# A third group of columns in seven products for eight, with two groups' sums kept in DRAM

## The chip, the cores and the metric

The kernel runs on one core of one Trainium2 chip. The metric is the device time of one execution in microseconds. TensorE (PE) multiplies, VectorE (DVE) and ScalarE (ACT) work on elements, GpSimd (POOL) and SyncE (SP) mostly issue transfers here.

## The reference

Two layers over 256 positions of width 2048, in float32. Each layer mixes positions (attention heads and gated groups, not touched here) and then runs the MLP that the change is about:

```python
h2 = rms_norm(x, norm2_g[l])
x = x + jnp.square(jax.nn.relu(h2 @ w_up[l])) @ w_down[l]
```

`w_up` is 2048 x 8192, `w_down` 8192 x 2048. After both layers a last norm is applied.

## The kernel before

**Precision and tiles.** A float32 product is made of three products of a reduced format: the high part of the weight with the high part of the other operand, low with high, high with low. Every 512 KB of weights is a tile `raw` of 128 x 1024; ScalarE copies it to its high part `hi` (L160) and VectorE subtracts that from `raw` to get the low part `lo` (L170). `x` is kept transposed, as 128 rows of 16 chunks.

**Steps.** The program is one list `steps`, and the loop at the end of `trunk` issues it: for each step the high and low parts of later tiles (low parts up to four tiles ahead of the step's first, with six `lo` and seven `hi` buffers), then loads, then the step's matmuls, then what follows it. A plain step of `transposed` (L391, L393, L395) takes one tile in 24 matmuls of 256 columns. `later` and `soon` put a piece of work off until so many tiles are done; `hook` ties one to a step. Each engine runs its own instructions in the order in which this loop issues them.

**The MLP.** It runs in rounds e = 0 to 8, called eighths here. Up to e = 7, eighth e makes 1024 hidden columns in 16 plain steps (0 to 15); every fourth step ends two chunks, which VectorE scales and clips (L733), ScalarE squares (L734) and both split into `half` (L629, L630). From e = 1 on, it also multiplies the hidden columns of e - 1 with 1024 rows of `w_down`, and `update` (L489) adds the result to `x`. A plain column block of 256 takes two plain steps.

**Seven products for eight.** A group is 512 of the 2048 output columns. `fast` multiplies its 1024 rows as a 2 x 2 block product with seven half-size products instead of eight (a Strassen-Winograd form). It takes two fast steps in each eighth, each with four tiles: two loaded (`Top`, `Bottom`) and two that VectorE makes from them (`Sums`, L210 to L214, written over the loaded ones). The hidden side needs sums too: `sums` (L747 to L750) and their splits (L629, L630 into `shared`). A fast step issues 36 matmuls; six of its seventh product are left to the step behind it (`left_over`).

Group 0 uses `fast` in all eight eighths and keeps its products in the four `aux` banks until the end. Group 1 uses it in eighths 1 to 7: two banks (`acc2`, `acc3`) and the free half bank hold five products all the time, and the sixth and seventh share whatever accumulator is free (`spare`), which is added up in SBUF in each eighth (`kept`, L803 and L805). When a group is complete, `combine` (L762 to L769) makes four blocks of the products and `turn_back` (L778) transposes them for `update`.

**The order around the change** is a table of positions: in eighths 2 to 7 the group 1 pair stands before steps 1 and 2, the group 0 pair before 6 and 13, and eight plain steps of `w_down` end the eighth:

```python
            at = {1: (7, 10, 14, 15), 8: (0, 2)}.get(e, (6, 13, 1, 2))
            for i, one in enumerate(rest):
                if quick and i in at:
                    steps.append(quick[at.index(i)])
                steps.append(one)
            if up:
                steps.extend(down)
```

Weights are loaded by SP; each load waits until the `lo` part of an earlier tile is made. POOL has nothing to do in the MLP.

Of the kernel before, what the change touches and what calls it, by code (L numbers as in the profile page):

```python
# [35 lines left out]
P = 128  # L36
# [4 lines left out]
NH = 8  # L41
# [19 lines left out]
FAST = (512, 512)  # L61
# [24 lines left out]
def trunk(ctx: ExitStack, tc: tile.TileContext, layout, xT, consts, gains, w, b_sp, w_sp, out):  # L86
# [6 lines left out]
    tp = ctx.enter_context(tc.tile_pool(name="tp", bufs=1))  # L93
    pacc = ctx.enter_context(tc.tile_pool(name="pacc", bufs=1, space=bass.MemoryType.PSUM))
# [12 lines left out]
    inner = ar[:, 0:2048].rearrange("p (k t) -> p k t", k=NH)  # L107
    blocks = ar[:, 2048:2048 + 6 * 256].rearrange("p (n c) -> p n c", n=6)
    kept = ar[:, 3584:3584 + 512]
# [288 lines left out]
    def fast(name, l, row0, col0, tiles, slots, fresh, last, done):  # L398
# [3 lines left out]

        o = []
        for p in range(2):
# [3 lines left out]
            def mm(p=p, top=top, bottom=bottom, upper=upper, lower=lower):  # L408
# [7 lines left out]
                def product(n, a, lower_rows, tt, b, cols):  # L416
                    for k in range(2):
                        xh, xl = (a[:, 4 * lower_rows + 2 * p + k, i, tt * P:(tt + 1) * P] for i in range(2))
                        hi, lo = b.hi[:, k, cols], b.lo[:, k, cols]
                        pe.matmul(o[n], lhsT=xh, rhs=hi, start=(p == 0 and k == 0 and n in fresh), stop=False,  # L420
                                  skip_group_check=True)
                        pe.matmul(o[n], lhsT=xh, rhs=lo, start=False, stop=False, skip_group_check=True)  # L422
                        pe.matmul(o[n], lhsT=xl, rhs=hi, start=False, stop=(last and p == 1 and k == 1),  # L423
                                  skip_group_check=True)
# [72 lines left out]
    def layer(l, n1, n2, n3, last):  # L497
# [261 lines left out]
        def combine(o, c, banks, final):  # L759
            p1, p2, p3, p5, p7, p6, p4 = o  # L760
            b1, u, c11, c12, c21, c22 = (blocks[:, n, :] for n in range(6))
            act.activation(b1, p1, AF.Copy)  # L762
            vec.tensor_tensor(u, b1, p6, op=OP.add)
            vec.tensor_tensor(c11, b1, p2, op=OP.add)
            vec.tensor_tensor(c22, u, p7, op=OP.add)
            vec.tensor_tensor(u, u, p5, op=OP.add)
            vec.tensor_tensor(c12, u, p3, op=OP.add)
            vec.tensor_tensor(c21, c22, p4, op=OP.subtract)
            vec.tensor_tensor(c22, c22, p5, op=OP.add)  # L769
            later(2, 1.5, lambda: turn_back(c, c11, c21, banks[0], final))  # L770
            later(2, 1.5, lambda: turn_back(c + 2, c12, c22, banks[1], final))

        def turn_back(c, first, second, bank, final):
            ps = bank()
            for j in range(2):
                for tt, src in enumerate((first, second)):
                    o = j * S + tt * P
                    pe.transpose(ps[:, o:o + P], src[:, j * P:(j + 1) * P], ident)  # L778
            later(0, 1.5, lambda: update(n3, c, ps, final, last))
# [6 lines left out]
        def slots_all():  # L786
            if not held:
                held.extend(h for _ in range(4) for h in halves(aux_bank()))
            return held[0:7]

        most, spare = [], [None]

        def slots_most():
            if not most:
                most.extend(h for i in (2, 3) for h in halves(acc_bank(i)))
            spare[0] = acc_bank(1 - bank_at[0])
            return most + halves(spare[0]) + held[7:8]

        def keep(e):

            def add(o):
                if e == 1:
                    act.activation(kept, spare[0], AF.Copy)  # L803
                else:
                    vec.tensor_tensor(kept, kept, spare[0], op=OP.add)  # L805
                if e == 7:
                    later(10, 1.5, lambda: combine(o[0:4] + halves(kept) + o[6:7], FAST[0] // P,
                                                  [lambda i=i: acc_bank(i) for i in (2, 3)], False))

            return add if e == 1 else lambda o: soon(1, lambda: add(o))  # L810

        base = len(steps)
        for e in range(9):
            up, down, quick, more = [], [], [], []
            if e < 8:
                up = collect(transposed, "w_up", l, 0, KC, e * 1024, 1024, from_hs, after_up(e), of=2)
            if e:
                w = sum(FAST[:1 + (e < 8)])
# [4 lines left out]
                quick = collect(fast, "w_down", l, (e - 1) * 1024, 0, hidden, slots_all, (0, 2, 4, 6) if e == 1 else (),  # L823
                                e == 8, (lambda o: later(1, 1.5, lambda: combine(o, 0, [aux_bank] * 2, True)))
                                if e == 8 else None)
                if e < 8:
                    quick += collect(fast, "w_down", l, (e - 1) * 1024, FAST[0], hidden, slots_most,
                                     (0, 2, 4) if e == 1 else (4,), e == 7, keep(e))
            rest = up or down
            at = {1: (7, 10, 14, 15), 8: (0, 2)}.get(e, (6, 13, 1, 2))  # L830
            for i, one in enumerate(rest):
                if quick and i in at:
                    steps.append(quick[at.index(i)])
                steps.append(one)
            if up:
                steps.extend(down)
# [137 lines left out]
```

## Time and profile before

| | |
|---|---|
| median of 3 runs | 2035.96 us (2035.77 to 2036.2) |
| the profiled execution | 2035.78 us, span 2034.0 us |
| granted TensorE clock | 0.997 |
| busy: PE, DVE, ACT, POOL | 2022.0, 1539.7, 1092.9, 68.5 us |
| MLP, layer 0 | from about 333 us to 1012 us of the span |
| one steady eighth | 84.5 to 84.6 us |
| read from HBM | 390.65 MB |

Busy time of PE is a poor measure of waits, because a matmul's record (277 ns) overlaps the next; the distance from one matmul to the next tells more. The bracket at a row of a timeline gives the idle time of that engine ahead of it and what ended it. Line numbers in the profile are those of the kernel before; in the order of the changed kernel the same lines stand four or five further down (L170 is L174 there, L489 is L494).

### The profile page before, as it was taken

Reading aid. Unit: us, or ns where it says so; the run is one execution under the profiler, and the core shown is the slowest. Engines: PE = TensorE matmul, PEld = TensorE weight load, DVE = VectorE, ACT = ScalarE, POOL = GpSimd, SP = SyncE. Lnnn points to the kernel's source line nnn. Section 1 sums busy time; section 2 is a strip of 40 time slices with the busy share of each in tenths; the row PEclk is TensorE's granted clock in tenths of the full one; section 3 lists DMA queues with packets and bytes.
Section 4 is the critical chain, followed back from the end, with each engine's and each line's share of the span. In section 5 each row is a group of like instructions: output and inputs, shape, how many; then the busy total and the mean of one; then the engine's idle time right before and its main releaser. Section 6 shows DMA issues by size and latency. Waiting matters only on the chain.

```text
span 2034.0 us, 40556 instructions
## 1 busy us (share of the span) xinstructions
PE 2022.0 (99%) x16914; PEld 1985.9 (98%) x16914; DVE 1539.7 (76%) x1906; ACT 1092.9 (54%) x1389; POOL 68.5 (3%) x90
## 2 busy tenths in 40 slices
PE   9999999999999999999999999999999999999997
PEld 8998999999999999999989989999999999999997
DVE  7666766788878787788866667658887788877886
ACT  7565444555555555555645554545554655546554
POOL 0002300000000000000000032000000000000000
PEclk9999999999999999999999999999999999999998
DMA  8545556465564655646564555555565555655653
GB/s 318 190 166 167 186 189 202 170 208 197 193 231 160 225 190 193 230 162 213 187 238 157 170 183 186 187 198 169 204 203 202 208 207 184 201 196 208 207 184 107
DMA packets 112136, 395.39 MB, mean 194 GB/s; under 512 B 12368, under 2 KB 16464, under 8 KB 111952
## 3 DMA queue, kind: packets, MB, share of 16 engines
q1 hardware_dynamic: 110800, 389.86, 56.2%
q8 instruction: 132, 2.16, 0.4%
q10 hardware_dynamic: 1152, 2.94, 0.4%
q14 instruction: 52, 0.43, 0.1%
HBM read 390.65 MB, written 2.10 MB: 193 GB/s over the span
## 4 chain that ended last, share of the span: by engine, by line
PE 99%; DVE 0%; ACT 0%; issue 0%; DVEq 0%
PE acc L391 25%; PE acc L395 25%; PE acc L393 25%; PE acc L451 3%; PE acc L449 3%; PE acc L450 3%; PE aux L420 3%; PE aux L423 3%; PE aux L422 3%; PE acc L423 2%; PE acc L422 2%; PE acc L420 2%; PE aux L675 0%; PE aux L577 0%; PE aux L619 0%; PE aux L606 0%
## 5 line engine op out<-in xcount | busy, mean ns | idle before, releaser
L160 ACT ACTIVATE hi<-raw 128x1024 fp32r<-128x1024 f32 (+1 forms) x801 | 807.8, 1048 | 463.5 <-DVE raw L214 210.9
L170 DVE TENSOR_TENSOR lo<-raw,hi 128x1024 fp32r<-128x1024 f32 (+1 forms) x801 | 944.9, 1216 | 46.8 <-ACT hi L160 31.3
L391 PE MATMUL acc<-hs,hi 128*128 128x256 f32 x2816 | 780.9, 277 | 0.0
L395 PE MATMUL acc<-hs,hi 128*128 128x256 f32 x2816 | 778.0, 276 | 0.0
L393 PE MATMUL acc<-hs,lo 128*128 128x256 f32 x2816 | 778.0, 276 | 0.0
L393 PEld LDWEIGHTS acc<-hs,lo 128*128 128x128 f32 x2816 | 528.8, 188 | 0.4 <-issue 0.2
L391 PEld LDWEIGHTS acc<-hs,hi 128*128 128x128 f32 x2816 | 528.7, 188 | 0.4 <-issue 0.2
L395 PEld LDWEIGHTS acc<-hs,hi 128*128 128x128 f32 x2816 | 528.6, 188 | 0.0
L391 PE MATMUL acc<-half,hi 128*128 128x256 f32 x1600 | 442.2, 276 | 0.0
L395 PE MATMUL acc<-half,hi 128*128 128x256 f32 x1600 | 441.7, 276 | 0.0
L393 PE MATMUL acc<-half,lo 128*128 128x256 f32 x1600 | 441.7, 276 | 0.0
L393 PEld LDWEIGHTS acc<-half,lo 128*128 128x128 f32 x1600 | 300.4, 188 | 0.0
L395 PEld LDWEIGHTS acc<-half,hi 128*128 128x128 f32 x1600 | 300.4, 188 | 0.0
L391 PEld LDWEIGHTS acc<-half,hi 128*128 128x128 f32 x1600 | 300.4, 188 | 0.0
L630 DVE TENSOR_TENSOR half<-ar,half 128x512 fp32r<-128x512 f32 x72 | 49.9, 693 | 92.8 <-ACT half L629 92.8
L733 DVE SCALAR_TENSOR_TENSOR ar<-acc,nR 128x512 f32<-128x512 f32 x64 | 44.1, 689 | 91.1 <-PE acc L395 91.1
L734 ACT ACTIVATE ar<-ar 128x512 f32<-128x512 f32 x64 | 40.5, 632 | 134.2 <-DVE ar L733 134.2
L489 DVE TENSOR_TENSOR x<-x,acc 128x512 f32<-128x512 f32 (+1 forms) x89 | 60.3, 678 | 66.7 <-PE acc L395 66.7
L449 PE MATMUL acc<-hi,hs 128*128 128x512 f32 x256 | 101.5, 397 | 0.0
L451 PE MATMUL acc<-hi,hs 128*128 128x512 f32 x256 | 100.6, 393 | 0.0
L450 PE MATMUL acc<-lo,hs 128*128 128x512 f32 x256 | 99.9, 390 | 0.0
L277 ACT ACTIVATE hs<-x,cols 128x256 fp32r<-128x256 f32 x64 | 29.2, 502 | 90.8 <-DVE x L489 90.0
(150 smaller groups left out, 2253.4 us busy)
## 6 DMA issues: line engine op xcount, KB each, us to landing
raw<-in_w SPq DMA_DIRECT2D x731, 512.0 KB, 4.5
raw<-in_w SPq DMA_DIRECT2D x10, 256.0 KB, 4.7
x<-in_xT SPq DMA_DIRECT2D x7, 256.0 KB, 5.4
out<-x SPq DMA_DIRECT2D x7, 256.0 KB, 3.1
shared<-in_b_sp ACTq DMA_DIRECT2D x2, 512.0 KB, 8.2
shared<-in_w_sp ACTq DMA_DIRECT2D x2, 512.0 KB, 9.8
con<-in_consts ACTq DMA_DIRECT2D x1, 512.0 KB, 7.6
x<-in_xT ACTq DMA_DIRECT2D x2, 128.0 KB, 3.9
```

Of the source, the lines that this page charges most:

```text
L160: act.activation(self.h[:, j * m:(j + 1) * m], self.raw[:, j * m:(j + 1) * m], AF.Copy)
L170: vec.tensor_tensor(lo[:, r], self.raw[:, r], self.h[:, r].bitcast(F32), op=OP.subtract)
L391: pe.matmul(o, lhsT=hi, rhs=xs[:, 0, :], start=(k0 + k == 0 and (two or cb == 0)), stop=False, skip_group_check=True)
L393: pe.matmul(o, lhsT=wt.lo[:, k, cb * P:(cb + 1) * P], rhs=xs[:, 0, :], start=False, stop=False, skip_group_check=True)
L395: pe.matmul(o, lhsT=hi, rhs=xs[:, 1, :], start=False, stop=last, skip_group_check=True)
L420: pe.matmul(o[n], lhsT=xh, rhs=hi, start=(p == 0 and k == 0 and n in fresh), stop=False, skip_group_check=True)
L422: pe.matmul(o[n], lhsT=xh, rhs=lo, start=False, stop=False, skip_group_check=True)
L423: pe.matmul(o[n], lhsT=xl, rhs=hi, start=False, stop=(last and p == 1 and k == 1), skip_group_check=True)
L449: pe.matmul(ps, lhsT=xh, rhs=hi, start=(k0 + k == 0), stop=False)
L450: pe.matmul(ps, lhsT=xh, rhs=lo, start=False, stop=False)
L451: pe.matmul(ps, lhsT=xl, rhs=hi, start=False, stop=(k0 + k == KC - 1))
L489: vec.tensor_tensor(xj, xj, ps[j][:, 0:S] if alone else pair(ps)[:, j, :], op=OP.add)
```

## The change

Group 2 (columns 1024 to 1535) now uses `fast` too, in eighths 2 to 7. The second projection's plain steps in these eighths are four in place of eight. Group 1 no longer stays in PSUM: both groups 1 and 2 start afresh in each eighth in `acc2`, `acc3` and the accumulator that is free; when a pair is done, ScalarE copies the three banks and the half bank of the seventh product to the SBUF buffer `stage` (L845, L836), and POOL issues a DMA of 128 x 1792 numbers that adds `stage` to the group's sums in DRAM (`far`, L813). Both groups share `stage`. Group 0's seventh product goes the same way (128 x 256), since its half bank is lent to group 2. In eighth 7, group 2's sums are added from DRAM into `stage` (L840), combined and turned back; then group 1's are read (L832) and combined. Combines and turns are put off with `soon` instead of `later`.

```diff
-FAST = (512, 512)
+ORDER = {1: ((7, 10), (13, 14)), 8: ((0, 2),)}
+USUAL = ((11, 14), (1, 2), (6, 7))
...
+    dp = ctx.enter_context(tc.tile_pool(name="dp", bufs=1, space=bass.MemoryType.DRAM))
...
-    inner = ar[:, 0:2048].rearrange("p (k t) -> p k t", k=NH)
-    blocks = ar[:, 2048:2048 + 6 * 256].rearrange("p (n c) -> p n c", n=6)
-    kept = ar[:, 3584:3584 + 512]
+    inner_flat = ar[:, 0:2048]
+    inner = inner_flat.rearrange("p (k t) -> p k t", k=NH)
+    stage, stage_one = ar[:, 2048:3840], ar[:, 3840:4096]
...
+        def combine(place, c, banks, o=None, then=None):
+            d1, d2, d3, d5, d7, d6, d4 = (place[:, 256 * n:256 * (n + 1)] for n in range(7))
+            p1, p2, p3, p5, p7, p6, p4 = o or (d1, d2, d3, d5, d7, d6, d4)
+            if o:
+                act.activation(d1, p1, AF.Copy)
+            vec.tensor_tensor(d2, d1, p2, op=OP.add)
...
+            soon(2, lambda: turn_back(c, d2, d4, banks[0], o is not None))
+            soon(3, lambda: (turn_back(c + 2, d3, d7, banks[1], o is not None), then and soon(1, then)))
...
+        def slots_other(g, banks):
+            seventh = sevenths()[g - 1]
+            banks[:] = [acc_bank(2), acc_bank(3), acc_bank(1 - bank_at[0])]
+            return [h for b in banks for h in halves(b)] + [seventh]
+
+        far = [dp.tile([P, 256 if g == 0 else 7 * 256], F32, name=f"far{l}{g}") for g in range(3)]
+
+        def put(e, g, src):
+            nc.gpsimd.dma_start(far[g], src, **({} if e == max(g, 1) else {"accum_op": OP.add}))
...
+        def other_done(e, g, banks):
+            here = [lambda i=i: acc_bank(i) for i in (2, 3)]
+
+            def back():
+                nc.gpsimd.dma_start(stage, far[1])
+                soon(3, lambda: combine(stage, 4, here))
+
+            def rest(o):
+                act.activation(stage[:, 1536:1792], o[6], AF.Copy)
+                if e < 7 or g == 1:
+                    put(e, g, stage)
+                else:
+                    nc.gpsimd.dma_start(stage, far[g], accum_op=OP.add)
+                    soon(4, lambda: combine(stage, 4 * g, here, then=back if g == 2 else None))
+
+            def f(o):
+                for i in (2, 0, 1):
+                    act.activation(stage[:, 512 * i:512 * (i + 1)], banks[i], AF.Copy)
+                soon(5, lambda: rest(o))
+            return f
...
+            quick = dict(quick)
+            for i, one in enumerate(up + down):
+                if i in quick:
+                    steps.append(quick[i])
                 steps.append(one)
```

**VectorE's order from one steady eighth into the next.** Before, from the four sums on; `raw` rows are the sums of weights, `shared` the splits of the hidden sums:

```order
L747 TENSOR_TENSOR ar<-ar 128x4x128
L748 TENSOR_TENSOR ar<-ar 128x4x128
L749 TENSOR_TENSOR ar<-ar 128x4x128
L750 TENSOR_TENSOR ar<-ar 128x4x128
L170 TENSOR_TENSOR lo<-raw,hi 128x1024
L489 TENSOR_TENSOR x<-x,acc_9123 128x512
L630 TENSOR_TENSOR shared<-ar,shared 128x2x256 x2
L170 TENSOR_TENSOR lo<-raw,hi 128x1024
L630 TENSOR_TENSOR shared<-ar,shared 128x2x256 x2
L170 TENSOR_TENSOR lo<-raw,hi 128x1024
L489 TENSOR_TENSOR x<-x,acc_9193 128x512
L170 TENSOR_TENSOR lo<-raw,hi 128x1024
```

The same place now:

```order
L752 TENSOR_TENSOR ar<-ar 128x4x128
L753 TENSOR_TENSOR ar<-ar 128x4x128
L754 TENSOR_TENSOR ar<-ar 128x4x128
L755 TENSOR_TENSOR ar<-ar 128x4x128
L187 TENSOR_TENSOR lo<-raw,hi 128x512
L494 TENSOR_TENSOR x<-x,acc_9357 128x512
L635 TENSOR_TENSOR shared<-ar,shared 128x2x256 x2
L217 TENSOR_TENSOR raw<-raw 128x2x256
L218 TENSOR_TENSOR raw<-raw 128x2x256
L174 TENSOR_TENSOR lo<-raw,hi 128x1024
L635 TENSOR_TENSOR shared<-ar,shared 128x2x256 x2
L214 TENSOR_TENSOR raw<-raw 128x2x256
```

The first fast step's tiles (L187, L217, L218, L214), which came behind four more low parts and two updates, now stand among the sums and their splits.

**VectorE's order from eighth 7 into eighth 8** (layer 0). Before, this place reads as the first list above; the combine of group 1 stood earlier, behind the square that follows step 7 of eighth 7. Now, from the last of the four sums on:

```order
L755 TENSOR_TENSOR ar<-ar 128x4x128
L217 TENSOR_TENSOR raw<-raw 128x2x256
L218 TENSOR_TENSOR raw<-raw 128x2x256
L770 TENSOR_TENSOR ar<-ar 128x256
L771 TENSOR_TENSOR ar<-ar 128x256
L772 TENSOR_TENSOR ar<-ar 128x256
L773 TENSOR_TENSOR ar<-ar 128x256
L774 TENSOR_TENSOR ar<-ar 128x256
L775 TENSOR_TENSOR ar<-ar 128x256
L778 TENSOR_TENSOR ar<-ar 128x256
L174 TENSOR_TENSOR lo<-raw,hi 128x1024
L494 TENSOR_TENSOR x<-x,acc_11477 128x512
```

Group 1's combine (L770 to L778) stands inside the preparation of eighth 8's first fast step. Group 2's stands in eighth 7 ahead of step 11, inside that of the second fast step of group 0.

80 lines of the change are left out of this document (33 added, 47 removed).

## The prediction

> **What bounds the kernel now.** I read the page first (busy shares, the chain that ended last), then the stretches of one eighth each, then VectorE's timeline from one eighth into the next, because the diff gives VectorE work and takes it from TensorE.
>
> ```profile
> PE 2022.0 (99%) x16914; PEld 1985.9 (98%) x16914; DVE 1539.7 (76%) x1906; ACT 1092.9 (54%) x1389; POOL 68.5 (3%) x90
> PE 99%; DVE 0%; ACT 0%; issue 0%; DVEq 0%
> ```
>
> TensorE is the chain. The columns of the next view are the stretch and its length, then busy time and instructions of PE, PEld, DVE, ACT, POOL, the granted clock, the DMA share and GB/s. The first two rows are steady eighths, the third is eighth 7.
>
> ```profile
> 609.10:693.60 84.50, 84.50 (x746) 84.50 (x745) 68.13 (x77) 45.47 (x52) 0.00 (x0) 1.00 0.58 200
> 693.60:778.20 84.60, 84.60 (x746) 84.60 (x746) 68.10 (x78) 45.47 (x52) 0.00 (x0) 1.00 0.57 198
> 862.80:948.20 85.40, 85.40 (x754) 85.40 (x753) 71.81 (x86) 45.60 (x53) 0.00 (x0) 1.00 0.56 190
> ```
>
> 84.5 us / 746 = 0.1133 us a matmul, at full clock and without holes. A plain step (24 matmuls) is then 2.72 us, a fast step (36, six more in the step behind it) 4.08 us, that next step 3.40 us. The 76% of VectorE over the span hides that it is 81% here, and that some of its idle time can't be used. Its timeline from the last square of one eighth (the start is also the end of PE's step 15) to the end of the next eighth's fast pair:
>
> ```profile
> 693.63 0.69 DVE L733 SCALAR_TENSOR_TENSOR ar<-acc,nR 128x512 f32<-128x512 f32 x1 [3.29 <-PE acc L395]
> 695.68 0.69 DVE L630 TENSOR_TENSOR half<-ar,half 128x512 fp32r<-128x512 f32 x1 [1.36 <-ACT half L629]
> 696.29 1.22 DVE L170 TENSOR_TENSOR lo<-raw,hi 128x1024 fp32r<-128x1024 f32 x1
> 697.43 0.69 DVE L747 TENSOR_TENSOR ar<-ar 128x512 f32<-128x512 f32 x1
> ...
> 700.21 1.22 DVE L170 TENSOR_TENSOR lo<-raw,hi 128x1024 fp32r<-128x1024 f32 x1
> 701.35 0.68 DVE L489 TENSOR_TENSOR x<-x,acc 128x512 f32<-128x512 f32 x1
> 701.94 1.29 DVE L630 TENSOR_TENSOR shared<-ar,shared 128x512 fp32r<-128x512 f32 x2
> 703.15 1.22 DVE L170 TENSOR_TENSOR lo<-raw,hi 128x1024 fp32r<-128x1024 f32 x1
> ...
> 709.95 0.69 DVE L489 TENSOR_TENSOR x<-x,acc 128x512 f32<-128x512 f32 x1 [0.91 <-PE acc L395]
> ...
> 718.48 0.68 DVE L183 TENSOR_TENSOR lo<-raw,hi 128x512 fp32r<-128x512 f32 x1
> 719.19 0.69 DVE L213 TENSOR_TENSOR raw<-raw 128x512 f32<-128x512 f32 x1
> 719.92 0.69 DVE L214 TENSOR_TENSOR raw<-raw 128x512 f32<-128x512 f32 x1
> 720.53 1.22 DVE L170 TENSOR_TENSOR lo<-raw,hi 128x1024 fp32r<-128x1024 f32 x1
> 721.78 0.69 DVE L210 TENSOR_TENSOR raw<-raw 128x512 f32<-128x512 f32 x1
> 722.51 0.69 DVE L211 TENSOR_TENSOR raw<-raw 128x512 f32<-128x512 f32 x1
> 723.12 3.66 DVE L170 TENSOR_TENSOR lo<-raw,hi 128x1024 fp32r<-128x1024 f32 x3
> 729.73 0.69 DVE L805 TENSOR_TENSOR ar<-ar,acc 128x512 f32<-128x512 f32 x1 [2.96 <-PE acc L423]
> ...
> 751.61 0.69 DVE L733 SCALAR_TENSOR_TENSOR ar<-acc,nR 128x512 f32<-128x512 f32 x1 [1.35 <-PE acc L395]
> ...
> 762.49 0.69 DVE L733 SCALAR_TENSOR_TENSOR ar<-acc,nR 128x512 f32<-128x512 f32 x1 [1.22 <-PE acc L395]
> 764.54 0.69 DVE L630 TENSOR_TENSOR half<-ar,half 128x512 fp32r<-128x512 f32 x1 [1.36 <-ACT half L629]
> 765.15 9.17 DVE L170 TENSOR_TENSOR lo<-raw,hi 128x1024 fp32r<-128x1024 f32 x8
> 778.19 0.69 DVE L733 SCALAR_TENSOR_TENSOR ar<-acc,nR 128x512 f32<-128x512 f32 x1 [3.87 <-PE acc L395]
> ```
>
> Prices on VectorE, from start to start. A plain low part: (9.17 - 1.22) / 7 = 1.14 us. A fast step: 723.12 - 718.48 = 4.64 us and two low parts more, 6.92 us. A square with its split: 696.29 - 693.63 = 2.66 us, of which 1.36 us waits for ScalarE in the middle (four times in an eighth, and nothing can slip in, since the queue is in order). The four sums of the hidden tile: 700.21 - 697.43 = 2.78 us; two of their splits 1.21 us; one update of x 0.59 us. So a fast step costs VectorE 6.92 us and TensorE 4.08; a plain one 1.14 against 2.72. VectorE may run at most five tiles ahead (six `lo` buffers), and here it waits for PE at each bracket above: 2.96, 1.35, 1.22, 3.87 and 0.91 us, 10.3 us in an eighth. This idle time is what the third group has to live on.
>
> **The change, part by part.** *The product that falls out.* Twelve group-eighths (eighths 2 to 7, two layers) go from 96 matmuls of 256 columns to 84: 12 x 12 x 0.1133 = -16.3 us, all on the chain. Turning a third group back adds 16 transposes:
>
> ```profile
> 924.52 0.42 DVE L763 TENSOR_TENSOR ar<-ar 128x256 f32<-128x256 f32 x1
> ...
> 926.89 0.42 DVE L769 TENSOR_TENSOR ar<-ar,acc 128x256 f32<-128x256 f32 x1
> 928.86 0.44 PE acc L778 x4
> ```
>
> Four transposes are 0.44 us: +1.8 us. TensorE alone would give -14.5 us. The seven operations of a combine take VectorE 926.89 - 924.52 and one more, 2.7 us.
>
> *VectorE over a steady eighth.* Four plain tiles (4.54 us) become two fast steps (13.84), two updates (1.18) and the addition at L805 (0.6) go: +7.5 us, against 84.5 - 12 x 0.1133 = 83.1 us of TensorE. All that VectorE then does, with the four waits of 1.36 us: 20 low parts 22.8, six fast steps 41.5, squares 10.6, sums and splits 5.2, updates 1.2, together 81.3 us. That is 98%: on average it fits, but only where the work stands evenly.
>
> *The border between two eighths* is where it doesn't. Between the last square and the next fast pair stood eight plain steps of the second projection; now there are four, so the cover is gone. VectorE has to do, from the square to the low part behind the pair: 2.66 + 3 low parts 3.41 + sums 2.78 + splits 2.42 + two updates 1.18 + two fast steps 13.84 = 26.3 us. TensorE gets there in five plain steps, fast, 3.40, fast: 13.6 + 4.08 + 3.40 + 4.08 = 25.2 us. The rows say the same another way: before, VectorE was done 33.2 us behind the square (723.12 + 3.66), 0.91 of it idle, and PE after 36.1; take away four plain tiles and two updates (5.7) there, 10.9 here, and VectorE is 1.3 us late where it had 2.96 us in hand. TensorE waits 1.1 us, at ten borders (2-3 to 6-7 in each layer): +11 us. Bounds: 0.5 (a first low part is wanted only at a step's second matmul) to 1.7 us each.
>
> *Eighth 7.* Both combines now fall into it. The second stands inside the same crowded border, before eighth 8's fast pair: 26.3 + 2.7 + three more updates 1.8 = 30.8 us of VectorE against 25.2 + 0.9 = 26.1 of TensorE, 4.7 us late. In layer 0 the update in between also makes the next layer's input:
>
> ```profile
> 980.25 0.69 DVE L489 TENSOR_TENSOR x<-x,acc 128x512 f32<-128x512 f32 x1 [0.21 <-PE acc L395]
> 981.52 0.88 DVE L281 SCALAR_TENSOR_TENSOR hs<-x,cols,hs 128x256 fp32r<-128x256 f32 x2 [0.58 <-ACT hs L277]
> 982.32 3.49 DVE L170 TENSOR_TENSOR lo<-raw,hi 128x1024 fp32r<-128x1024 f32 x3
> ```
>
> 982.32 - 980.25 is 2.07 in place of 0.59 us: 6.2 us. Both layers +11 us, between 7 and 17. The first combine (2.7, two updates 1.2) has 0.9 us of transposes and the 1.8 us that the eighth has left: 1.2 us late at least, 2.2 where the fast step behind it waits; taken 2, +4 us, from 0 to 8.
>
> *ScalarE, DMA, queues.* The copies of L845 and L836 are 3.5 operations on a group's banks. Their nearest rows, ScalarE's timeline and the DMA issues (KB each, us to landing):
>
> ```profile
> 436.49 0.60 ACT L803 ACTIVATE ar<-acc 128x512 f32<-128x512 f32 x1 [1.74 <-PE acc L423]
> 436.99 3.90 ACT L160 ACTIVATE hi<-raw 128x1024 fp32r<-128x1024 f32 x4
> raw<-in_w SPq DMA_DIRECT2D x731, 512.0 KB, 4.5
> ```
>
> Two groups add some 4 us to ScalarE's 45.5, the two fast steps 3: far from full. But the three copies stand in the queue until PE ends the pair and hold back the high parts behind them by 1.7 us; two steps are ready by then, so this is mostly hidden: +2 us in all, from 0 to 4. SP issues as many loads as before. POOL has nothing else to do here; each transfer waits for the copy only, and who waits for it is the next group's first copy (one buffer). 896 KB at the rate of a load (512 KB in 4.5 us) take 7.9 us; the buffer is wanted again two plain steps and a fast pair later, 17 us. Taken as hidden; the upper end is a rival.
>
> The sum, against the profiled execution's 2035.8 us (span 2034.0; the median of the runs is 0.2 higher): -16.3 + 1.8 + 11 + 11 + 4 + 2 = +13.5, 2049 us. With all low ends -2 (2034), with all high ends +32 (2067). I take 2049 since the border's shortage comes out of two readings.
>
> **The rivals.** *TensorE stays the pace.* VectorE's 81.3 us are less than 83.1, and 10.3 us of its idle time stand against 7.5 of new work; should its lead carry over the borders, TensorE loses nothing: 2035.8 - 14.5 = 2021.3 us, and with a few microseconds at the border to eighth 8 up to 2031. It decides below 10.4 us of waits in all (against 28 in my sum), about 0.5 us a border and 2.5 for the combines of each layer. Against it: the square waits for PE, so a lead can't be saved up over it.
>
> *The waits eat the saving and no more*: 2032 to 2040 us, no change that can be told (0.2% of this time, 4 us, is about what a measurement can tell).
>
> *The sums in DRAM are late.* A sum reads the source, reads the old value and writes the new one; at three times a load's bytes it takes 23.7 us, not 7.9. Then ScalarE stands 7 us at the second group's copies, and PE, which needs one of these banks 3.40 us behind the pair, some 3 us in each of 12 eighths, +36; twice the bytes (15.8) would cost only in eighth 7, where the combine stands 9.5 us behind the issue of its sum (two plain steps and a fast one), 6 us in each layer. 2063 to 2085 us. For it speaks that no row shows a transfer from POOL or a sum; against it a DMA share of 0.58.
> The Trainium skill (SBUF — State Buffer, section "SBUF: two separate sides") has a rule by which this would happen by itself: descriptors of a DMA from GpSimd's queue are written by GpSimd, which is locked out while VectorE runs in a two-port mode. By it the sums would starve beside a VectorE that is 98% busy, and the time would be at the top of this rival. The rows above (0.69 us for 512 elements, 1.22 for 1024: 1.04 ns an element, no halved rate) show no such mode in these operations, and the section says two-input operations disturb only a GpSimd operation that reads SBUF; so it adds little to the chance.
>
> That the change doesn't remove the products is excluded by the order: 144 matmuls fewer, 16 transposes more.
>
> **How the numbers follow.** VectorE late at the borders, 2040 to 2063: 0.45; TensorE's pace, 2021 to 2031: 0.28; the middle: 0.15; late sums: 0.12. Faster 0.28, same 0.15, slower 0.57. For eight in ten, 2022 to 2064; the likeliest case alone 2040 to 2063.
>
> **What the profile after would show.** Right: PE's waits at the pairs of steps 1 and 2 released by VectorE's low parts (L174), about 1 us an eighth; steady eighths of 84 to 85 us with 12 matmuls fewer; VectorE's wait at what was L805's place gone; 5 us lost between eighths 7 and 8. Wrong: steady eighths of 83 us; or copies at L845 released by a DMA, and combines at L770 that wait for one, for which I have no price from a row.

## The result and the profile after

The changed kernel takes 2084.31 us (median of 4 runs, 2084.13 to 2087.77) against 2036.08 (2035.77 to 2036.61, 4 runs): a ratio of 1.0241, 95% interval 1.0223 to 1.0258. It is slower by 48 us; the prediction was 2049 and ended its range at 2064.

The page of the changed kernel, busy times and the chain that ended last (the code has moved: L170 is now L174, L489 L494, L630 L635, L733 L738, L391 to L395 L395 to L399, L423 L428, L778 L787):

```profile
PE 2045.0 (98%) x16786; PEld 1989.5 (96%) x16786; DVE 1632.8 (78%) x2034; ACT 1174.6 (56%) x1551; POOL 103.3 (5%) x134
PE 71%; DVE 16%; ACT 5%; DMA 4%; issue 4%; DVEq 0%; ACTq 0%
```

TensorE has 128 matmuls fewer in all (144 of 256 columns fewer, 16 transposes more) and 23 us more of busy time. It is no longer the whole chain: VectorE holds 16% of it, ScalarE 5%, DMA 4%. The stretches of two steady eighths and of eighth 7, with the columns as in the prediction:

```profile
622.11:708.87 86.76, 85.89 (x734) 84.20 (x733) 75.26 (x86) 52.75 (x67) 2.58 (x3) 1.00 0.69 220
708.87:796.17 87.30, 85.91 (x734) 84.35 (x733) 75.35 (x86) 51.78 (x65) 2.59 (x3) 1.00 0.67 215
883.60:974.17 90.57, 87.11 (x743) 85.33 (x742) 79.07 (x96) 51.84 (x65) 3.19 (x4) 1.00 0.68 220
```

With 12 matmuls fewer than before an eighth takes 2.3 to 2.7 us longer, at the full granted clock. 734 matmuls at 0.1133 us would take 83.2. The largest waits of TensorE's weight loads (PEld) in the changed kernel (engine and line, what it waited for, us in total, times, longest):

```profile
PEld acc L397 <- DVE lo L174: 16.2, 43, 1.5
PEld acc L427 <- DVE lo L174: 7.9, 24, 1.2
PEld aux L427 <- DVE lo L174: 7.3, 9, 1.3
PEld acc L787 <- DVE ar L775: 5.9, 4, 1.9
PEld aux L787 <- DVE ar L777: 2.4, 2, 1.3
```

Before, no wait of PE or PEld in the MLP was put down to a low part. These rows say who is waited for, but not what a wait costs. For that I took the starts of the MLP's 256-column matmuls and counted what each distance from one to the next has over 0.1133 us. Distances above 0.158 (stops) come to 47.3 us, against 3.4 before; the small excesses below that to 14.3, against 4.6; the time around other matmuls grew by 11.1, of which 1.8 is for the transposes. With 144 matmuls fewer (-16.3) that is +48.4, the whole difference. TensorE's timeline from the first fast step of the pair behind a border into the plain step after it, some rows of it:

```profile
638.18 0.39 PE L427 MATMUL acc<-lo,shared 128*128 128x256 f32 x1 [0.36 <-DVE lo L174]
638.41 0.28 PE L428 MATMUL acc<-hi,shared 128*128 128x256 f32 x1
638.53 0.28 PE L425 MATMUL acc<-hi,shared 128*128 128x256 f32 x1
638.64 0.28 PE L427 MATMUL acc<-lo,shared 128*128 128x256 f32 x1
...
639.92 0.39 PE L427 MATMUL acc<-lo,shared 128*128 128x256 f32 x1
640.14 0.28 PE L428 MATMUL acc<-hi,shared 128*128 128x256 f32 x1
...
641.05 0.39 PE L397 MATMUL acc<-hs,lo 128*128 128x256 f32 x1 [0.16 <-DVE lo L174]
641.27 0.28 PE L399 MATMUL acc<-hs,hi 128*128 128x256 f32 x1
```

Each time a matmul that takes a low part comes late, two of them with a wait named, and the next one comes 0.22 us behind it, not 0.11. Such a stop is paid twice: 98 of the stops have that second 0.11 us, 10.7 us in all (part of the 47.3), which no row of waits shows.

### The profile page after: what moved, and what is told of

Read it like the earlier page. It is cut to its first block, busy times and chain, and to the rows that moved or that the text cites. A ratio compares the mean times of both kernels' runs of the same rounds, so it can differ in the third digit from the quotient of the medians.

```text
span 2082.4 us, 40770 instructions
## 1 busy us (share of the span) xinstructions
PE 2045.0 (98%) x16786; PEld 1989.5 (96%) x16786; DVE 1632.8 (78%) x2034; ACT 1174.6 (56%) x1551; POOL 103.3 (5%) x134
## 4 chain that ended last, share of the span: by engine, by line
PE 71%; DVE 16%; ACT 5%; DMA 4%; issue 4%; DVEq 0%; ACTq 0%
PE acc L397 16%; PE acc L399 16%; PE acc L395 16%; DVE lo L174 6%; DMA raw<-in_w 4%; PE acc L454 3%; PE acc L456 3%; PE acc L455 3%; PE acc L427 3%; PE acc L428 2%; PE acc L425 2%; ACT hi L164 2%; PE aux L427 2%; PE aux L428 2%; PE aux L425 2%
## 5 line engine op out<-in xcount | busy, mean ns | idle before, releaser
L164 ACT ACTIVATE hi<-raw 128x1024 fp32r<-128x1024 f32 (+1 forms) x825 | 831.4, 1049 | 465.1 <-DVE raw L218 185.4
L174 DVE TENSOR_TENSOR lo<-raw,hi 128x1024 fp32r<-128x1024 f32 (+1 forms) x825 | 970.4, 1213 | 87.9 <-ACT hi L164 71.1
L395 PE MATMUL acc<-hs,hi 128*128 128x256 f32 x2816 | 782.0, 278 | 0.0
L399 PE MATMUL acc<-hs,hi 128*128 128x256 f32 x2816 | 779.1, 277 | 0.0
L395 PEld LDWEIGHTS acc<-hs,hi 128*128 128x128 f32 x2816 | 529.5, 188 | 0.3 <-issue 0.2
L399 PEld LDWEIGHTS acc<-hs,hi 128*128 128x128 f32 x2816 | 528.6, 188 | 0.0
L397 PE MATMUL acc<-half,lo 128*128 128x256 f32 x1216 | 337.2, 277 | 3.5 <-DVE lo L174 3.5
L395 PE MATMUL acc<-half,hi 128*128 128x256 f32 x1216 | 337.7, 278 | 0.0
L399 PE MATMUL acc<-half,hi 128*128 128x256 f32 x1216 | 336.8, 277 | 0.0
L397 PEld LDWEIGHTS acc<-half,lo 128*128 128x128 f32 x1216 | 229.0, 188 | 4.1 <-DVE lo L174 4.1
L395 PEld LDWEIGHTS acc<-half,hi 128*128 128x128 f32 x1216 | 229.4, 189 | 0.0
L399 PEld LDWEIGHTS acc<-half,hi 128*128 128x128 f32 x1216 | 228.9, 188 | 0.0
L635 DVE TENSOR_TENSOR half<-ar,half 128x512 fp32r<-128x512 f32 x72 | 49.8, 692 | 94.4 <-ACT half L634 94.4
L427 PE MATMUL acc<-lo,shared 128*128 128x256 f32 x416 | 119.7, 288 | 3.1 <-DVE lo L174 2.6
L428 PE MATMUL acc<-hi,shared 128*128 128x256 f32 x416 | 115.5, 278 | 0.0
L425 PE MATMUL acc<-hi,shared 128*128 128x256 f32 x416 | 115.5, 278 | 0.0
L813 POOL DMA_DIRECT2D far<-ar x38 | 31.2, 821 | 1380.0 <-ACT ar L836 720.5
```

The costliest lines, as they stand in the source:

```text
L164: act.activation(self.h[:, j * m:(j + 1) * m], self.raw[:, j * m:(j + 1) * m], AF.Copy)
L174: vec.tensor_tensor(lo[:, r], self.raw[:, r], self.h[:, r].bitcast(F32), op=OP.subtract)
L395: pe.matmul(o, lhsT=hi, rhs=xs[:, 0, :], start=(k0 + k == 0 and (two or cb == 0)), stop=False, skip_group_check=True)
L397: pe.matmul(o, lhsT=wt.lo[:, k, cb * P:(cb + 1) * P], rhs=xs[:, 0, :], start=False, stop=False, skip_group_check=True)
L399: pe.matmul(o, lhsT=hi, rhs=xs[:, 1, :], start=False, stop=last, skip_group_check=True)
L428: pe.matmul(o[n], lhsT=xl, rhs=hi, start=False, stop=(n in last and p == 1 and k == 1), skip_group_check=True)
```

## The experiments

All times stand beside medians of 2035.84 to 2036.16 for the kernel before. Unless noted, each kernel is the changed one with the edit shown. "By place" means that the stops are sorted by their distance from the last square of an eighth.

**Are the transfers late, or the copies in the way?**

`e1_no_adds` makes only each group's first transfer to DRAM; the later sums are left out:

```
-            nc.gpsimd.dma_start(far[g], src, **({} if e == max(g, 1) else {"accum_op": OP.add}))
+            if e == max(g, 1):
+                nc.gpsimd.dma_start(far[g], src)
```


> Only the first transfer of each group's sums to DRAM is kept, all later adding transfers are left out (the sums are then incomplete). Theory A (VectorE sets the pace of the steady eighths, and loses 2.7 us in each by standing behind ScalarE, whose queue is held at the copies until TensorE ends a pair): VectorE's waits for late weights, 0.9 us an eighth, are all that can go: 2074 to 2084 us. Theory B (the transfers that add in DRAM delay the weights): most of the 63 us of waits go, 2030 to 2045 us.

2077.22 us, ratio 1.0202 (1.0173 to 1.0232), as A said: the sums in DRAM cost about 7 us; 41 us stay. By place these 7 us are stops at group 0's pair, in eighths 3 to 6 8.3 us in the changed kernel and 0.1 here. The sums make the weights late there: loads of weights issued 60 to 75 us behind the square land after 7.2 us (median, eighths 3 to 7) in the changed kernel, after 5.5 here. VectorE's waits for them, first the changed kernel, then this one:

```profile
DVE raw L218 <- DMA raw<-in_w: 7.9, 10, 1.4
DVE raw L218 <- DMA raw<-in_w: 3.0, 2, 2.3
```

`e2_no_copies` leaves the three bank copies out in all but a group's first eighth:

```
-                for i in (2, 0, 1):
+                for i in (2, 0, 1) if e == max(g, 1) else ():
```


> The three bank copies on ScalarE are made only in the first eighth of each group; the copy of the seventh product and all transfers stay (so the sums are of old numbers). Theory A: the two waits of 1.36 us that VectorE has behind the copies go in 11 to 12 eighths, 27 to 33 us: 2051 to 2058 us. Theory B: the transfers are the same, 2080 to 2086 us.

2066.40 us, 1.0149 (1.012 to 1.0179): 18 us less, where A expected 27 to 33. By place it is clear-cut: at the pair behind the ten borders 17.2 us stay of 17.4, at the pairs of groups 2 and 0 in twelve eighths 6 of 18. So the copies do not cause the stops at the border, but most of the others. How, ScalarE's and VectorE's timelines of the changed kernel show at one pair:

```profile
645.76 2.96 ACT L164 ACTIVATE hi<-raw 128x1024 fp32r<-128x1024 f32 x3 [1.52 <-DVE raw L215]
649.14 1.57 ACT L845 ACTIVATE ar<-acc 128x512 f32<-128x512 f32 x3 [0.42 <-PE acc L428]
650.59 2.02 ACT L164 ACTIVATE hi<-raw 128x1024 fp32r<-128x1024 f32 x2
```

```profile
645.56 4.79 DVE L174 TENSOR_TENSOR lo<-raw,hi 128x1024 fp32r<-128x1024 f32 x4
651.69 2.36 DVE L174 TENSOR_TENSOR lo<-raw,hi 128x1024 fp32r<-128x1024 f32 x2 [1.35 <-ACT hi L164]
```

The copies wait for PE's pair and then take 1.57 us; the next high part starts behind them at 650.59, and VectorE stands 1.35 us for it. This happens twice in an eighth, in a queue that has little time to spare. VectorE's wait for high parts over the whole run, in the kernel before and in the changed one:

```profile
DVE lo L170 <- ACT hi L160: 31.3, 30, 3.7
DVE lo L174 <- ACT hi L164: 71.1, 56, 4.4
```

`e7_copies_later` keeps all the work and moves the copies one step back:

```
-            def f(o):
+            def copies():
                 for i in (2, 0, 1):
                     act.activation(stage[:, 512 * i:512 * (i + 1)], banks[i], AF.Copy)
+
+            def f(o):
+                soon(1, copies)
                 soon(5, lambda: rest(o))
```


> The changed kernel with the three bank copies on ScalarE issued one step later, behind one more high part, the same work. Hold theory (the copies stand in front of the high parts until PE ends the pair, and a VectorE without slack passes this on): the 18 us that leaving most copies out gained come back in good part, 2064 to 2074. Rival (the copies' own time on ScalarE counts, or their place does not): 2080 to 2087.

2075.08 us, 1.0191 (1.0161 to 1.022), a gain of 9. VectorE's wait for high parts is 31.7 us, as before the change. In its timelines the copies start without a wait, and VectorE makes six low parts in a row there:

```profile
652.60 1.06 ACT L164 ACTIVATE hi<-raw 128x1024 fp32r<-128x1024 f32 x1 [2.20 <-DVE lo L187]
653.56 1.55 ACT L845 ACTIVATE ar<-acc 128x512 f32<-128x512 f32 x3
```

```profile
644.82 7.06 DVE L174 TENSOR_TENSOR lo<-raw,hi 128x1024 fp32r<-128x1024 f32 x6
```

So the hold was real and its place was the fault. The stops at group 0's pair in eighths 3 to 6 are all gone, although the loads ahead of it are as late as in the changed kernel (7.3 us). These 8 us thus need both the late loads and the hold, and the gains of `e1_no_adds` and `e2_no_copies` can't be added up. The gain is half of that of `e2_no_copies`; new stops, mostly of 0.4 to 1.1 us an eighth, stand about 55 us behind the square, where TensorE now waits for a copy:

```profile
PE acc L395 <- ACT ar L845: 5.3, 9, 1.4
```

**What in VectorE's work counts, and where.** `e4_no_weight_sums` and `e9_no_border_sums` leave out the weight subtractions of a single group, of the third (its pair at steps 6, 7) and of the second (the pair at steps 1, 2 behind the border):

```
-            if self.second:
+            if self.plain:
+                pass
+            elif self.second:
...
-            upper, lower = Sums(top, bottom, False), Sums(top, bottom, True)
+            upper, lower = (Sums(top, bottom, second, col0 == 1024) for second in (False, True))  # e4; e9: col0 == 512
```


> The four subtractions of weights on VectorE are left out in group 2 (its products are then of other numbers); all else stays as in the changed kernel. Theory A: VectorE has 5.4 us less in each of 12 eighths, and TensorE's pace (83.1 us an eighth) comes back: 2040 to 2048 us. Theory B: 2080 to 2086 us.

> The changed kernel without the eight subtractions of weights (5.8 us of VectorE an eighth) in the second group, whose pair is the one at steps 1, 2 behind the border; the earlier run without them in the third group (steps 6, 7) gained nothing, 2083.7. Border theory (VectorE's work between the square and this pair is what PE waits for there, about 2.0 us in each of ten eighths): these stops go, 2060 to 2067. Rival (VectorE's time is not what counts, here as little as in the third group): 2079 to 2086.

The third group's made no difference, 2083.69 us (1.0234, 1.0205 to 1.0264). The stops at its own pair went from 5.6 us to 0.2, but VectorE only came to the hold sooner: its wait for high parts rose from 71.1 to 121.9 us, right behind this group's copies from 23.0 to 63.9, and the next pair, group 0's, gained nothing (12.5 and 13.3 us). All stops fell by 6 us, the small excesses rose by 3.5. The second group's gave 2066.60 (1.015, 1.012 to 1.0179), the 18 us expected, and by place as expected: no stop is left at that pair in any of the ten eighths. VectorE's wait for high parts rose as much here, to 122.5 us, so that this wait alone doesn't tell the time. One eighth of that run:

```profile
619.80:704.87 85.07, 84.72 (x735) 83.93 (x734) 69.40 (x79) 51.86 (x65) 2.57 (x3) 1.00 0.69 221
```

`e10_no_sums_later` leaves out all weight subtractions (`plain` always true) and has the copies of `e7_copies_later`:

> The changed kernel without any subtraction of weights (VectorE is relieved of 17 us in each eighth) and with the three bank copies one step later. Theory (VectorE's work at the pairs and the hold at the copies are all that PE stops for inside the eighths): eighths of 83.0 to 83.5 us instead of 86.7 to 87.5, what is left is eighth 7 and the border behind it, 2036 to 2045. Rival (something else, such as the transfers or PE's pitch, sets 86 us): 2055 to 2075.

2030.93 us (8 runs), 0.9976 (0.9964 to 0.9987), below the expectation and below the kernel before. Its eighth:

```profile
618.00:701.30 83.30, 83.30 (x734) 83.30 (x734) 59.27 (x62) 52.55 (x65) 2.57 (x3) 1.00 0.72 227
```

No stop is left in the steady eighths, with the same transfers and copies and a higher DMA share than in the changed kernel. So VectorE's work and the hold at the copies together account for the loss inside the eighths; the late loads cost only where VectorE has no time left. This kernel is no version of the change, since its products lack the sums. `e12_no_second_combine` leaves group 1's combine out (`then=None`):

> The changed kernel without the second combine (group 1's sums are not turned back and not added to x). The prediction gave that combine 4.7 us in one layer and 6.2 in the other; the stretch from eighth 7 to the end of eighth 8 in fact lost 8.6 us in each against its matmuls. Theory (all of that is the combine in the crowded border): 2066 to 2072, with the 16 transposes' 1.8 us in it. Rival (the border behind eighth 7 loses by its pair, as the others do, and the combine little): 2076 to 2084.

2078.34 us, 1.0208 (1.0178 to 1.0237): 6 us in all, 1.8 of them for its transposes. Stops at the last eighth's pair fell from 8.9 to 6.9 us. The rival was nearer: most of it is the pair that is not covered, not the combine ahead of it.

**Can the order or another engine carry it?** `e6_later_pair` gives the border one more plain step of cover:

```
-USUAL = ((11, 14), (1, 2), (6, 7))
+USUAL = ((11, 14), (2, 3), (6, 7))
```


> The changed kernel with the second group's pair at steps 2, 3 instead of 1, 2: 2.72 us more of cover behind the square, the same work. Border theory: the stops at that pair, about 2.0 us in each of ten eighths, go, 20 us in all, and the others stay: 2062 to 2068. Rival (VectorE has no time left at all, so the stops only move to the next pairs): 2080 to 2087.

2096.26 us, 1.0295 (1.0262 to 1.0328), worse than both. The stops at the moved pair are all gone; in eighths 3 to 7 those at group 2's pair, at most 0.5 us an eighth in the changed kernel, are now 2.0 to 2.5, and those at group 0's, 0.2 to 2.1 there, are 1.0 to 4.2. The stops move, and more than the whole comes back.

`e16_spaced` and `e18_spaced_at_once` spread the six fast steps, with the copies one step later and at once:

```
-USUAL = ((11, 14), (1, 2), (6, 7))
+USUAL = ((10, 14), (1, 3), (5, 7))
```


> The changed kernel with the copies one step later and the fast steps spread out: group 1 at steps 1 and 3, group 2 at 5 and 7, group 0 at 10 and 14, the same work. A fast step costs VectorE 2.84 us more than PE, a plain one gives back 1.58, 2.26 where it carries six products. Theory (VectorE's 81.3 us would fit into 83, it is the bunching that stops PE): 2050 to 2064. Rival (the sum is what does not fit, the stops only move): 2073 to 2085.

> The spread order of the fast steps once more (group 1 at 1 and 3, group 2 at 5 and 7, group 0 at 10 and 14), with the copies at once as in the changed kernel: in the spread run with late copies PE waited up to 2.9 us for the copy of the bank that it needs right behind steps 3 and 7, twice an eighth. Theory (bunching is what stops PE, the sum of VectorE's work fits): 2050 to 2070. Rival (the sum does not fit, and the order hardly matters): 2078 to 2095.

2131.02 us (1.0467, 1.0436 to 1.0497) and 2172.53 (1.0669, 1.0638 to 1.07). The first was spoiled by a wait of its own, TensorE for the copy of the bank that it needs behind steps 3 and 7:

```profile
PE acc L395 <- ACT ar L845: 28.1, 10, 2.9
```

The second has no such wait and is still far worse, and neither theory holds for it. Two waits of VectorE in its trace are much longer than in the changed kernel, where the first is 7.9 us and the second absent: for loads of weights, and at a combine for the sums from DRAM:

```profile
DVE raw L218 <- DMA raw<-in_w: 35.0, 10, 5.1
DVE ar L770 <- DMA ar<-far: 17.8, 2, 9.0
```

With this order the transfers are late, then; why, and what else makes an even spacing cost more than pairs, is open. `e17_spaced_all` adds the hidden sums on GpSimd and the last pair at steps 3 and 6 to `e16_spaced`:

> All that should relieve VectorE at once: copies later, hidden sums on GpSimd, fast steps spread out, and the last eighth's pair at steps 3 and 6 instead of 0 and 2. Theory (bunching and border are the whole loss, TensorE alone would give 2021): eighths of 83 to 84 us, 2030 to 2045. Rival (VectorE's sum does not fit either way): 2055 to 2075.

2161.94 us, 1.0619 (1.0588 to 1.0649).

Three more give VectorE's work to GpSimd: the weight subtractions (`e8_sums_on_gpsimd`); the low parts of the plain second-projection steps, with late copies (`e11_lows_on_gpsimd`); the four hidden sums, with late copies (`e13_hidden_sums_gpsimd`):

```
-                vec.tensor_tensor(b.right(), b.right(), t.left(), op=OP.subtract)   # e8: all four
+                nc.gpsimd.tensor_tensor(b.right(), b.right(), t.left(), op=OP.subtract)
...
+            for step in down if e < 8 else ():                                      # e11
+                step[0].low_on = nc.gpsimd
...
-            vec.tensor_tensor(a22, a21, a22, op=OP.add)                             # e13: all four
+            nc.gpsimd.tensor_tensor(a22, a21, a22, op=OP.add)
```


> The changed kernel with the four sums of weights of every fast step on GpSimd: VectorE is relieved of 2.8 us in each of six fast steps an eighth, GpSimd gets about 1.2 us for each sum (half of its 2.43 us for 128x1024), 29 us an eighth. Theory (VectorE's share is what PE waits for everywhere): PE becomes the pace in the eighths, 2025 to 2045. Rival (latency: four sums in a row take 4.9 us instead of 2.9 between the low parts that they wait for and those that wait for them, and VectorE stands in between): stops stay or grow, 2075 to 2110.

> The changed kernel with the copies one step later and the low parts of the plain steps of the second projection (four in an eighth, just behind the square) on GpSimd: VectorE is relieved of 4.6 us at the border, GpSimd gets 4 of about 2.5 to 3 us in the 10.9 us of these steps. Border theory: VectorE is in time at the pair of steps 1, 2 and at that of the last eighth, eighths of 83.5 to 84.5, 2038 to 2056. Rival (GpSimd's low parts come too late themselves, as the sums on GpSimd did): 2072 to 2100.

> The changed kernel with the copies one step later and the four sums of the hidden tile (2.8 us of VectorE behind the square) on GpSimd, where they should take about 5 us (4 x 1.25, GpSimd's 128x1024 took 2.43). The fast pair that needs them comes 13.6 us behind the square. Border theory (2.0 us of stops in each border are work of VectorE): against the 2075.1 of the copies alone 2052 to 2060. Rival (the longer way over GpSimd delays the splits behind them, and the stops stay): 2072 to 2082.

2227.22 (1.0938, 1.0906 to 1.097), 2112.01 (1.0373, 1.0343 to 1.0403) and 2098.18 us (1.0305, 1.0275 to 1.0335): the rivals each time, worse than expected. GpSimd's groups of `e8_sums_on_gpsimd`, and its timeline and VectorE's in `e13_hidden_sums_gpsimd`:

```profile
L217 POOL TENSOR_TENSOR raw<-raw 128x512 f32<-128x512 f32 x84 | 157.1, 1871 | 868.6 <-DVE lo L187 868.6
L215 POOL TENSOR_TENSOR raw<-raw 128x512 f32<-128x512 f32 x84 | 144.0, 1714 | 6.6
```

```profile
627.09 2.20 POOL L752 TENSOR_TENSOR ar<-ar 128x512 f32<-128x512 f32 x1 [2.60 <-DVE half L635]
629.36 1.62 POOL L753 TENSOR_TENSOR ar<-ar 128x512 f32<-128x512 f32 x1
631.06 1.29 POOL L754 TENSOR_TENSOR ar<-ar 128x512 f32<-128x512 f32 x1
632.43 1.30 POOL L755 TENSOR_TENSOR ar<-ar 128x512 f32<-128x512 f32 x1
```

```profile
633.05 1.83 DVE L635 TENSOR_TENSOR shared<-ar,shared 128x512 fp32r<-128x512 f32 x2 [2.62 <-ACT shared L634]
```

The four hidden sums take 6.4 us on GpSimd and 2.8 on VectorE; VectorE, in order, then stands 2.62 us for what it gave away. Work in the middle of a chain was not relieved by a slower engine.

**A second pitch of TensorE.** `e3_two_groups` has the new scheme for group 1 only; `e5_two_groups_later` also moves its pair to steps 2 and 3; `e19_two_groups_copies_later` has the copies of `e7_copies_later` in place of that:

```
-USUAL = ((11, 14), (1, 2), (6, 7))
+USUAL = ((6, 13), (1, 2))                    # e3, e19; e5: (2, 3)
...
-                if e < 7 or g == 1:
+                if e < 7:
```


> Only the way of the sums is changed against the kernel before: group 1's sums go to DRAM and come back in eighth 7, group 2 stays with plain steps, and the pairs stand where they stood before (1, 2 and 6, 13). Theory A: VectorE has some 10 us of waits for TensorE in each eighth, so a wait of 1.4 us behind the copies costs nothing: 2033 to 2040 us. Theory B: half of the transfers, about half of the loss: 2055 to 2065 us.

> The run with two groups (2061.99 us) lost its 26 us without waits: its trace shows 256-column matmuls 0.1177 us apart instead of 0.1133, from one short stop of PE at 577.6 us (the step behind the fast pair at steps 1, 2) to a stop at 932, and again from 1599 to 1948. Here the same two groups, the pair one plain step later (2, 3), so that PE should not stop there. Theory P (a stop switches PE's pitch, nothing else costs): no such stretch, 2036 to 2042. Rival (the transfers or the combine through DRAM themselves slow PE): 2058 to 2064.

> Two groups, as in the run of 2061.99 us, with the bank copies one step later. There ScalarE stood 3.46 us at the copies behind the pair of eighth 2, VectorE then 4.38 us, PE stopped for 0.1 us at 577.6 and ran at 0.1177 us a matmul up to 932, and the same again in the second layer. Theory P (that stop brings the slow pitch, the pitch is the whole loss): no stop, no such stretch, 2033 to 2040. Rival (the slow pitch comes from the transfers or from the order of the instructions, stop or not): 2055 to 2063.

`e3_two_groups` took 2061.99 us, 1.0128 (1.0095 to 1.016), where the transfers' theory put it. But its trace has as many matmuls as before and no wait of PE that explains 26 us. Three stretches of 20 us, of this run, of `e19_two_groups_copies_later` and of the kernel before:

```profile
610.00:630.00 20.00, 20.00 (x173) 20.00 (x172) 15.26 (x21) 8.84 (x12) 0.00 (x0) 1.00 0.59 190
```

```profile
610.00:630.00 20.00, 20.00 (x179) 20.00 (x178) 17.52 (x23) 9.91 (x13) 0.00 (x0) 1.00 0.56 169
```

```profile
610.00:630.00 20.00, 20.00 (x179) 20.00 (x178) 17.76 (x24) 9.71 (x13) 0.00 (x0) 1.00 0.42 140
```

PE is full in all three, the granted clock is 1.00, and the first does 173 matmuls where the others do 179: 0.1177 us apart instead of 0.1133. 3005 matmuls in a row run so, from 578 us to 931, and again from 1599 to 1952. The first stretch begins here:

```profile
577.40 0.28 PE L395 MATMUL acc<-hs,hi 128*128 128x256 f32 x1
577.61 0.39 PE L397 MATMUL acc<-hs,lo 128*128 128x256 f32 x1
577.83 0.28 PE L399 MATMUL acc<-hs,hi 128*128 128x256 f32 x1
```

The stop at 577.61 has a history in the same run, ScalarE first, then VectorE:

```profile
561.91 1.58 ACT L845 ACTIVATE ar<-acc 128x512 f32<-128x512 f32 x3 [3.46 <-PE acc L428]
```

```profile
564.46 2.36 DVE L174 TENSOR_TENSOR lo<-raw,hi 128x1024 fp32r<-128x1024 f32 x2 [4.38 <-ACT hi L164]
```

`e5_two_groups_later` told nothing on it: the moved pair brought stops of its own, 65 us of them, 2105.04 us, 1.0338 (1.0302 to 1.0374). `e19_two_groups_copies_later` did: with the same transfers, but without the hold there is no stop and no such stretch, and the time is 2038.39 us (8 runs), 1.0012 (1.0001 to 1.0024). The hold of 3.46 us, on an engine at half load, thus goes with a loss of 24 us. The slow stretch begins at a stop of 0.1 us in each layer, but that this stop is the cause is not shown. That a stop as such does this is not so: `e15_before_one_stop` puts a stop into the kernel before,

```
+            for _ in range(self.delay):
+                vec.tensor_tensor(lo, self.raw, self.raw, op=OP.subtract)
...
+            if e == 2:
+                rest[2][0].delay = 4
```


> The kernel before, with 4 repeated subtractions (4.8 us of VectorE, their result overwritten) ahead of one low part in each layer, that of the plain step behind the second fast step of the pair at steps 1, 2 in eighth 2. VectorE has some 3 us in hand there, so PE should stop for about 2 us in each layer. Theory P (a stop can leave PE at 0.1177 us a matmul instead of 0.1133 until it stops again): besides the 2 x 2 us a stretch of slow pitch of up to 350 us, 12 to 15 us, in one or both layers, 2046 to 2066. Rival (a stop costs its length and no more): 2037 to 2041.

and takes 2042.75 us, 1.0032 (1.0017 to 1.0048). Two stops (5.3 us in the waits), behind each of them a dozen matmuls at half rate (see the end), and no stretch of the second pitch. Most of the long stretches that I found begin at a stop at the second matmul of a step behind a fast pair's second half, as in `e3_two_groups`, and end at a later stop; what decides which stops do it is open.

## Why the prediction was wrong

The direction and the mechanism were right, and VectorE's sum too: 81.3 us an eighth were worked out with the four waits of 1.36; the row has 75.3 busy, with them 80.7. What was mis-sized, in microseconds over the run:

| step of the prediction | forecast | in the trace | shown by |
|---|---|---|---|
| products and transposes | -14.5 | -14.5 | counts of matmuls |
| pair behind ten borders | +11 (5 to 17) | +17.4 | `e9_no_border_sums`: -17.7 |
| copies on ScalarE, "mostly hidden", and first combine | +2 and +4 | +18.2 at the pairs of groups 2 and 0, 12 of it gone without the copies | `e2_no_copies`: -18 in all |
| border behind eighth 7, second combine | +11 | +8.9 at its pair, +9.3 around the transposes (about 2.0 ahead of the first combine's, 4.4 the second's, 2.3 group 0's) | `e12_no_second_combine`: -6, of which 1.8 transposes |
| TensorE's pitch | not in the sum | +9.7 | starts of the matmuls |
| sums in DRAM | 0, "taken as hidden" | 7, at group 0's pair | `e1_no_adds`: -7 |

(The last row lies within the 18.2; the rest add up to 49, about the difference of 48.)

*The copies* are the step that failed most: +2 us was given to them, and 12 us of stops go with them. The prediction saw that they hold back the high parts by 1.7 us and called this hidden because two steps were ready by then. It asked only whether TensorE has enough ahead at that moment. But VectorE, which it had just found 98% full, has little idle time to give: it stands 1.35 us, twice an eighth, 32 us over the twelve, and makes up only a part of that before the next pair.

*The transfers* were taken as hidden because no copy would wait for them. None did; but the loads of weights, for which the prediction counted only that they are as many as before, land later beside them, and 8 us of the same stops need this too.

*The border* was at its upper bound, 1.74 us and not 1.1. The account took the lateness once, at the end of the pair; the trace has up to five stops in it, most with 0.11 us more at the next matmul, at most 0.55 in all. That is about the difference; no run tests it alone.

*Eighth 7* came near in its sum, 8.9 and 4.4 us against 11, but the price was put on the wrong thing: the second combine costs 4 us in `e12_no_second_combine` where about 9 of the 11 were its share, and the uncovered pair costs most of the rest.

*TensorE's pitch* was taken as 0.1133 us throughout; parts of the changed kernel run at 0.1177, which no term of the sum has.

*What was right:* the waits named L174 and lay at the pairs; L805's wait is gone. The sums in DRAM themselves were in time (loads, then sums):

```profile
raw<-in_w SPq DMA_DIRECT2D x731, 512.0 KB, 4.8
far<-ar POOLq DMA_DIRECT2D x24, 896.0 KB, 7.3
```

7.3 us to landing where 7.9 were worked out, and no copy at L845 waited for a transfer. The time lies in the range of the rival *the sums in DRAM are late* (2063 to 2085), but by chance: without the later sums 41 of the 48 us stay.

The Trainium skill's rule by which descriptors from GpSimd starve while VectorE runs in a two-port mode (SBUF — State Buffer, section "SBUF: two separate sides") does not show here: these transfers landed in 7.3 us beside a VectorE that was 87% busy. The sign of the steady eighths was passed on the far side: 84 to 85 us were forecast, 83 would have shown the theory wrong, and 86.8 came. *TensorE stays the pace* gave 2021 to 2031; with VectorE relieved of 17 us an eighth and the copies one step later (`e10_no_sums_later`) the run took 2030.93. So that limit exists, but VectorE and the hold keep the change from it.

## What to carry to other kernels

When a change fills a second engine to 98% of the pace, its waits begin to cost, also those that were hidden before: price every instruction and every transfer that can stand in front of its inputs, on all queues, and not only the work that is added. A saving on the bounding engine is worth what the next engine has to spare in the places where the work stands, and here moving the fast steps about without taking work away only moved the stops, or added to them. Before a long wait is sought for a loss, compare the distance between back-to-back instructions with that of the kernel before.

## What was not expected of the hardware

- TensorE has two pitches for the same back-to-back matmuls of 256 columns, 0.1133 and 0.1177 us, at a granted clock of 1.00 and without a wait in any row. Up to 3005 matmuls in a row kept the slower one. In the changed kernel and in `e3_two_groups` the pitch changes only at stops; in `e16_spaced` it also does at a single distance of 0.12 us.
- A matmul that waited for its operand is followed by the next after 0.22 us, not 0.11 (98 times in the changed kernel).
- A stop of 2.12 us was followed, 1.3 us later, by matmuls at half the rate. TensorE's timeline at that stop, in `e18_spaced_at_once`, and two stretches behind it:

```profile
677.68 0.39 PE L427 MATMUL acc<-lo,shared 128*128 128x256 f32 x1 [2.12 <-DVE lo L174]
```

```profile
679.40:682.40 3.00, 3.00 (x16) 3.00 (x16) 2.93 (x5) 0.35 (x1) 0.00 (x0) 0.50 1.02 236
684.00:687.00 3.00, 3.00 (x29) 3.00 (x29) 2.95 (x4) 2.37 (x3) 0.00 (x0) 1.00 0.98 282
```

16 matmuls in 3 us at a granted clock of 0.50, then 29 at 1.00. This run lost some 24 us so, in 16 such stretches, the changed kernel 1.3 in one. The Trainium skill (TensorE: Matmul & The Clock Gate, section "Why this matters for your kernels") advises no gaps of TensorE above about 3 us; here the half rate came behind shorter ones.
- GpSimd's operations on 128 x 512 took 1.29 to 2.20 us in the chain of `e13_hidden_sums_gpsimd` and 1.38 to 1.87 on average in `e8_sums_on_gpsimd`, where VectorE takes 0.69.
